# Gate tiles from one DRAM buffer per token chunk, the first of them on GpSimd's queue, and routing steps over more expert blocks

## The chip, the cores and the metric

The kernel runs on one core of a Trainium2 chip. The metric is the time of one execution on the device, in microseconds; lower is better. The profile is of one execution of the same program.

## The reference

Two layers over 512 tokens of 1024 numbers. Layer 0 mixes with a gated linear recurrence, layer 1 with attention that forgets; after each mixer stands a PEER feed-forward, which is what the change is about:

```
q = (xc @ q_w).reshape(TOKEN_CHUNK, PEER_HEADS, 2, PEER_HALF)
s1, s2 = scores of q against two sets of 128 subkeys, for 8 heads
v1, i1 = lax.top_k(s1, 16); v2, i2 = lax.top_k(s2, 16)
top_s, top_c = lax.top_k(all sums of a v1 and a v2, 16)
expert = e1 * 128 + e2                    # 16384 experts, 16 a head
g = jax.nn.softmax(top_s, axis=-1)
act = gelu(einsum('thkd,td->thk', take(expert_u, expert), xc))
out = einsum('thk,thkd->td', g * act, take(expert_v, expert))
```

Everything is float32.

## The kernel before

`peer` (L612) is called once per layer. It treats the four chunks of 128 tokens in two ways. For three of them (`nd` = 3) the experts are computed densely: for each of 128 blocks of 128 experts, the first product (u, 24 matmuls of 384 columns, names `pacc`, L334 to L336), a Gelu, a multiplication by a dense matrix of gates that is zero for experts not chosen, and the second product (v, `vacc`, L949). For the fourth chunk, GpSimd gathers the rows of the chosen experts (L855) and VectorE multiplies them (L864, L876). Every float32 operand of a matmul is split in two parts, by ScalarE (`whi`, L211) and VectorE (`wlo`, L212).

The work of one layer stands in stages:

1. Queries, scores and the search for the best 16.
2. A loop over 44 blocks of experts whose first product is computed ahead (`first_up`, L632) and kept in DRAM (`ascr`). Beside the blocks runs background work: after each block `bg.pump(GP)` gives it credit, and each step of a generator that runs takes the cost that it yields. The background is, for four chunks, `route` (L768, four steps of VectorE work per chunk, names `ge`, `j`, `e`), and then, for three chunks, `dense_gates` (L787): each has 8 groups; a group makes masks on VectorE (`p`, L829 and L832; `pg`, L840), 32 small matmuls on TensorE (`gps`, L816), copies on ScalarE (`st`, L818) and a store to the DRAM buffer `gscr` (L819).
3. A loop over the 128 blocks (L961), six blocks ahead with the first product (`expert_in`). It reads the gates back from `gscr` as gate tiles (`gtile`) of 8 blocks of experts, 1536 KB each (L919), multiplies (`gated`, L935), splits (`wh`, `wl`) and runs `expert_out`. GpSimd's gathers begin once the first gated product is there (L860).

The tile framework orders each engine's instructions by priorities that it works out while building, so an instruction may stand ahead of code that was written earlier. SP's queue loads weights (`wraw`, L148) and, before the change, all gate tiles. ScalarE's queue carries the stores of `gscr` and `ascr`. GpSimd's queue carries the gathers. A load from a DRAM tile waits for the stores to that tile.

Of the kernel before, what the change touches and what calls it, by code (L numbers as in the profile page):

```python
# [4 lines left out]
F32 = mybir.dt.float32  # L5
# [30 lines left out]
NEARLY = sum(EARLY)  # L36
PUMPS = ((4.05, 1.25), (3.75, 1.15))
AHEAD = 6
GP = 4.5
GSCALE = 32768.0  # L40
M0 = 14
M2 = 18
# [12 lines left out]
def pad(g, pool, size):  # L55

    g.nc.gpsimd.memset(pool.tile([128, size // 4], F32, name="pad", bufs=1), 0.0)
# [519 lines left out]
def stored(k):  # L577


    k -= AHEAD // 2  # L580
    n, m = NFIRST // 2, PK // 2 - AHEAD // 2
    return k >= 0 and (k + 1) * n // m > k * n // m
# [29 lines left out]
def peer(g, norm_fn, u, v, grow_fn, between, nd, cost):  # L612


    tc, nc = g.tc, g.nc
    V, A, T = nc.vector, nc.scalar, nc.tensor
    ND = nd * 128
    NB = ND // 16
    gscr = g.dram.tile([NB, 128, 128, 16], F32, name="gscr", tag="gscr")
    ascr = g.dram.tile([NFIRST, 128, ND], F32, name="ascr", tag="ascr")  # L620
    with pool(tc, name="pk", bufs=1) as pk:
        hn = pk.tile([128, D], F32, name="hn")
# [100 lines left out]
        def fold(x, last):  # L723

            n = TOPK
            while n > 2:
                V.tensor_tensor(x[:, 0:n // 2, :], x[:, 0:n:2, :], x[:, 1:n:2, :], op=OP.add)  # L727
                n //= 2
            V.tensor_tensor(last, x[:, 0, :], x[:, 1, :], op=OP.add)

        def route_half(t, q):

            if q == 0:
                routes[t] = [rt.tile([128, PH * TOPK], F32, name=f"e{w}", tag=f"e{w}", bufs=TC) for w in range(2)]
            e = routes[t]
            shp = [128, TOPK, HK]
            hs = slice(q * QH, q * QH + QH)
            ks = slice(q * HK, q * HK + HK)
            posb = rt.tile([128, HK], BF, name="posb", tag="posb")
            pin = tc.keep_in_program_order if q == 0 else lambda x: x  # L740
            pin(V.tensor_copy(posb, pos[:, t, hs].rearrange("p a b -> p (a b)")))
            f1 = rt.tile([128, QH, TOPK], F32, name="f1", tag="f1")
            pin(V.tensor_copy(f1, idxs[0][:, t, hs]))
            d1 = rt.tile([128, QH, TOPK], F32, name="d1", tag="d1")
            V.tensor_copy(d1[:, :, 0:1], f1[:, :, 0:1])
            V.tensor_sub(d1[:, :, 1:], f1[:, :, 1:], f1[:, :, :-1])
            tab = []
            for w, src in enumerate((d1, idxs[1][:, t, hs])):
                x = rt.tile(shp, BF, name=f"tab{w}", tag=f"tab{w}")
                A.activation(x.rearrange("p r (h k) -> p r h k", h=QH),  # L750
                             src.rearrange("p h r -> p r h").unsqueeze(3).to_broadcast([128, TOPK, QH, TOPK]), AF.Copy)
                tab.append(x)
            ge = rt.tile(shp, BF, name="ge", tag="ge")
            ge2 = rt.tile(shp, BF, name="ge2", tag="ge2")
            V.tensor_tensor(ge, posb.unsqueeze(1).to_broadcast(shp), thr, op=OP.is_ge)
            V.tensor_tensor(ge2, ge, row, op=OP.mult)
            V.tensor_tensor(ge, ge, tab[0], op=OP.mult)
            fold(ge, e[0][:, ks])
            yield 4.4
            j = rt.tile([128, HK], BF, name="j", tag="j")  # L760
            fold(ge2, j)
            V.tensor_sub(j, posb, j)
            V.tensor_tensor(ge, j.unsqueeze(1).to_broadcast(shp), col, op=OP.is_equal)
            V.tensor_tensor(ge, ge, tab[1], op=OP.mult)
            fold(ge, e[1][:, ks])
            yield 4.4

        def route(t):  # L768

# [17 lines left out]
        def dense_gates(t, pu, pw, psum, todo):  # L787

            e1, e2, gt = routes[t]
            tp = psum.tile([128, 4, 128], F32, name="tp", tag="tp", bufs=1)
            for i, s in enumerate((e1, e2, gt)):
                T.transpose(tp[:, i, :], s, g.ident)
            shp = [128, 128, 8]
            edup = [pu.tile(shp, F16, name=f"edup{w}", tag=f"edup{w}") for w in range(2)]
            for w in range(2):
                A.activation(edup[w], tp[:, w, :].unsqueeze(2).to_broadcast(shp), AF.Copy)
            gp = [pu.tile([128, 128], F16, name=f"gp{i}", tag=f"gp{i}") for i in range(2)]
            V.tensor_scalar(gp[0], tp[:, 2, :], GSCALE, None, op0=OP.mult)  # L800
            V.scalar_tensor_tensor(gp[1], tp[:, 2, :], GSCALE, gp[0], op0=OP.mult, op1=OP.subtract)
            gdup = []
            for i in range(2):
                d = pu.tile(shp, F16, name=f"gdup{i}", tag=f"gdup{i}")
                A.activation(d, gp[i].unsqueeze(2).to_broadcast(shp), AF.Copy)
                gdup.append(d)
            yield 1.5

            def products(n, p2, pg):
                st = pw.tile([128, 128, 16], F32, name="st", tag="st", bufs=3)  # L810
                for q in range(4):
                    gps = psum.tile([128, 4, 128], F32, name="gps", tag="sps", bufs=4)
                    for r in range(4):
                        tk_ = q * 4 + r
                        for i in range(2):
                            T.matmul(gps[:, r, :], p2[:, tk_, :, :].rearrange("p a b -> p (a b)"), pg[i][:, :, tk_, :],  # L816
                                     start=(i == 0), stop=(i == 1))
                    A.activation(st[:, :, q * 4:q * 4 + 4].rearrange("p e t -> p t e"), gps, AF.Copy, scale=1.0 / GSCALE)  # L818
                nc.scalar.dma_start(gscr[n], st)  # L819

            shp = [128, 16, 16, 8]
            it = iota_e.unsqueeze(2).to_broadcast(shp)
            for b in range(8):
                bs = slice(b * 16, b * 16 + 16)

                def spread(x):
                    return x[:, bs, :].unsqueeze(1).to_broadcast(shp)
                p2 = pw.tile(shp, F16, name="p2", tag="p2")
                V.tensor_tensor(p2, iota_e.unsqueeze(1).to_broadcast(shp),  # L829
                                edup[1][:, bs, :].unsqueeze(2).to_broadcast(shp), op=OP.is_equal)  # L830
                p1 = pu.tile(shp, F16, name="p1", tag="p1")
                V.tensor_tensor(p1, it, spread(edup[0]), op=OP.is_equal)  # L832
                yield 2.4
                if todo:
                    products(*todo.pop())
                    yield 0.1
                pg = []
                for i in range(2):
                    x = pw.tile(shp, F16, name=f"pg{i}", tag=f"pg{i}")
                    V.tensor_tensor(x, p1, spread(gdup[i]), op=OP.mult)  # L840
                    pg.append(x)
                    yield 1.15
                todo.append((t * 8 + b, p2, pg))
            if t == nd - 1:
                products(*todo.pop())
# [40 lines left out]
        with pool(tc, name="ups", bufs=1, space=PSUM) as psum:  # L886
# [6 lines left out]
            with pool(tc, name="pu", bufs=1) as pu, pool(tc, name="pw", bufs=2) as pw:  # L893
                todo = []
                bg = Background(*[route(t) for t in range(TC)], *[dense_gates(t, pu, pw, psum, todo) for t in range(nd)])
                for c in FIRST[NEARLY:]:
# [3 lines left out]
                    if c in FIRST[NEARLY + 1:NEARLY + 6:4]:  # L900
                        natural(g, psum, h, TC - 1, hn, FIRST.index(c) // (NEARLY + 5))
                    bg.pump(GP)
                bg.finish()
# [3 lines left out]
        with pool(tc, name="vw", bufs=2) as vw, pool(tc, name="vps", bufs=2, space=PSUM) as psum:  # L907
            gguard = pool(tc, name="gat", bufs=8)
            gat = gguard.__enter__()
            env["gat"], env["vw"] = gat, vw  # L910
            pad(g, vw, 384)
            g.stream.third = (vw, 2)
            bg = Background(*late)
            acc = [[psum.tile([128, 512], F32, name=f"vacc{t}{d}", bufs=1) for d in range(2)] for t in range(nd)]
            ready, ins, gts = {}, {}, {}

            def gate_tile(n):
                gts[n] = vw.tile([128, NB, 8, 16], F32, name="gtile", tag="gtile")
                nc.sync.dma_start(gts[n], gscr[:, :, n * 8:n * 8 + 8, :].rearrange("b p e t -> p b e t"))  # L919

            def expert_in(c):

                if c and c % 8 == 0:
                    gate_tile(c // 8)
                ins[c] = vw.tile([128, ND], F32, name="at2", tag="at2", bufs=AHEAD + 2)
                if stored(c // 2):
                    nc.scalar.dma_start(ins[c], ascr[FIRST.index(c)])
                else:
                    A.activation(ins[c], proj_t(g, psum, h, ND), AF.Gelu)  # L929
# [22 lines left out]
            def pump(i):  # L952
                bg.pump(cost[1] if stored(i // 2) else cost[0])

            for i in range(AHEAD):
                if i == 3:
                    gate_tile(0)
                expert_in(i)
                if i > 3:
                    gated(i - 4)()  # L960
# [425 lines left out]
```

## Time and profile before

| what | us |
|---|---|
| median of 3 runs | 3155.22 |
| lowest and highest | 3146.97, 3159.86 |
| the profiled execution, its own time | 3146.6 |
| its span, from first to last instruction | 3144.8 |
| PE busy | 3050.0 |
| VectorE (DVE) busy | 2583.9 |
| ScalarE (ACT) busy | 1457.9 |
| GpSimd (POOL) busy | 959.7 |

In the profile's rows PE is the matmul engine and PEld its weight loads; "x" is a count; what stands in brackets or after "|" is the idle time ahead of an instruction and what ended it. Each stage of layer 0 has a twin in layer 1, some 1610 us later: routing runs from 460 us to 541 and from 2071 to 2152, the dense gates from there to 692 and 2303, and the loop over 128 blocks follows.

### The profile page before, as it was taken

The numbers are of one execution on the slowest core, as the hardware profiler recorded it, in microseconds if no ns is written. First come the engines' busy times: TensorE is split into PE (matmuls) and PEld (weight loads), VectorE is DVE, ScalarE is ACT, GpSimd is POOL, SyncE is SP. The second block draws the span as 40 slices with busy tenths as digits, with TensorE's granted clock in tenths as the row PEclk, the third lists the DMA queues.
The fourth block names the chain that finished last, engine by engine and source line by source line (L and its number), as shares of the span: only waits on it lengthen the run. The fifth ranks groups of instructions, "written<-read, shape, count | busy, mean of one in ns | idle before, by whom it ended". The sixth has DMA issues, their size and how long they took to land.

```text
span 3144.8 us, 44367 instructions
## 1 busy us (share of the span) xinstructions
PE 3050.0 (97%) x16192; PEld 2681.3 (85%) x16192; DVE 2583.9 (82%) x5297; ACT 1457.9 (46%) x2109; POOL 959.7 (31%) x845
## 2 busy tenths in 40 slices
PE   6998999999999999999999999999999999999999
PEld 5876899998888888888777778899998888888887
DVE  7876899887988988888569876999869788888884
ACT  4763236883333333333458743257853333333332
POOL 1001440006644245542011102410037344544430
PEclk9998999999999999999999999999999999999999
DMA  6545334779999999997332243346699999999983
GB/s 264 155 172 170 113 131 168 268 271 400 409 377 362 365 361 355 362 343 285 126 119 82 95 143 123 104 167 222 248 359 411 360 374 340 343 340 347 355 311 117
DMA packets 304780, 818.98 MB, mean 260 GB/s; under 512 B 27824, under 2 KB 156848, under 8 KB 276016
## 3 DMA queue, kind: packets, MB, share of 16 engines
q1 hardware_dynamic: 173104, 389.83, 34.8%
q0 software_dynamic: 89408, 321.43, 26.8%
q10 hardware_dynamic: 42048, 104.88, 9.0%
q8 instruction: 127, 2.08, 0.3%
q14 instruction: 93, 0.76, 0.1%
HBM read 735.03 MB, written 81.02 MB: 259 GB/s over the span
## 4 chain that ended last, share of the span: by engine, by line
PE 60%; DVE 15%; issue 10%; DMA 6%; POOL 5%; ACT 4%; SPq 0%; POOLq 0%; DVEq 0%; ACTq 0%
PE vacc L949 22%; PE pacc L334 9%; PE pacc L336 9%; PE pacc L335 9%; POOL rows L855 4%; PE gps L816 3%; DVE wlo L212 3%; DMA wraw<-in_l_v_dram 2%; DVE rows L864 1%; DVE mw L177 1%; DVE tk L652 1%; ACT whi L211 1%; DVE ge L727 1%; DMA at<-ascr 1%; DVE idxs L651 1%
## 5 line engine op out<-in xcount | busy, mean ns | idle before, releaser
L211 ACT ACTIVATE whi<-wraw 128x1024 fp32r<-128x1024 f32 (+1 forms) x646 | 663.3, 1034 | 598.4 <-PE pacc L335 349.7
L334 PE MATMUL pacc<-hhi,whi 128*128 128x384 f32 (+1 forms) x2632 | 926.2, 352 | 8.5 <-ACT at L929 5.0
L336 PE MATMUL pacc<-hhi,wlo 128*128 128x384 f32 (+1 forms) x2632 | 921.3, 350 | 3.5 <-DVE wlo L212 3.5
L335 PE MATMUL pacc<-hlo,whi 128*128 128x384 f32 (+1 forms) x2632 | 919.6, 349 | 0.0
L212 DVE TENSOR_TENSOR wlo<-wraw,whi 128x1024 fp32r<-128x1024 f32 (+1 forms) x580 | 700.5, 1211 | 187.7 <-ACT whi L211 187.2
L949 PE MATMUL vacc<-wlo,wh 128*128 128x512 f32 x1536 | 605.2, 394 | 0.7 <-DVE wlo L212 0.7
L949 PE MATMUL vacc<-whi,wh 128*128 128x512 f32 x1536 | 602.1, 392 | 0.0
L949 PE MATMUL vacc<-whi,wl 128*128 128x512 f32 x1536 | 596.6, 388 | 0.5 <-DVE wl L942 0.4
L334 PEld LDWEIGHTS pacc<-hhi,whi 128*128 128x128 f32 x2632 | 495.9, 188 | 39.0 <-ACT at L929 5.6
L336 PEld LDWEIGHTS pacc<-hhi,wlo 128*128 128x128 f32 x2632 | 495.1, 188 | 30.2 <-DVE wlo L212 5.4
L335 PEld LDWEIGHTS pacc<-hlo,whi 128*128 128x128 f32 x2632 | 495.9, 188 | 29.2 <-issue 1.7
L939 ACT ACTIVATE wh<-at 128x384 fp32r<-128x384 f32 x256 | 134.0, 525 | 768.0 <-DVE at L935 469.2
L855 POOL DMA_INDIRECT rows<-in_l_v_dram,ei x256 | 360.5, 1408 | 382.1 <-DVE accg L876 342.9
L855 POOL DMA_INDIRECT rows<-in_l_u_dram,ei x256 | 367.9, 1437 | 264.4 <-DVE rows L864 212.5
L949 PEld LDWEIGHTS vacc<-whi,wl 128*128 128x128 f32 x1536 | 288.3, 188 | 66.1 <-DVE wl L942 1.8
L949 PEld LDWEIGHTS vacc<-whi,wh 128*128 128x128 f32 x1536 | 288.2, 188 | 61.4
L949 PEld LDWEIGHTS vacc<-wlo,wh 128*128 128x128 f32 x1536 | 288.8, 188 | 53.5 <-DVE wlo L212 1.1
L876 DVE SCALAR_TENSOR_TENSOR accg<-rows,act,accg 128x1024 f32<-128x1024 f32 x254 | 324.8, 1279 | 0.5
L864 DVE SCALAR_TENSOR_TENSOR rows<-rows,hn 128x1024 f32<-128x1024 f32 x256 | 304.8, 1219 | 12.6 <-DMA rows<-in_l_u_dram,ei 12.6
L935 DVE TENSOR_TENSOR at<-at,gtile 128x384 f32<-128x384 f32 x256 | 140.7, 552 | 131.8 <-DMA at<-ascr 122.1
L818 ACT ACTIVATE st<-gps 128x512 f32<-128x512 f32 x192 | 186.0, 1111 | 35.7 <-PE gps L816 35.7
L212 POOL TENSOR_TENSOR wlo<-wraw,whi 128x1024 fp32r<-128x1024 f32 (+1 forms) x66 | 134.9, 2054 | 192.0 <-ACT whi L211 192.0
(281 smaller groups left out, 3367.6 us busy)
## 6 DMA issues: line engine op xcount, KB each, us to landing
wraw<-in_l_uT_dram SPq DMA_DIRECT2D x128, 1024.0 KB, 7.1
wraw<-in_l_v_dram SPq DMA_DIRECT2D x128, 1024.0 KB, 9.4
gscr<-st ACTq DMA_DIRECT2D x48, 1024.0 KB, 5.1
gtile<-gscr SPq DMA_DIRECT2D x32, 1536.0 KB, 16.1
mw<-in_l_ffn_mw_dram POOLq DMA_DIRECT2D x48, 512.0 KB, 3.6
ascr<-at ACTq DMA_DIRECT2D x112, 192.0 KB, 2.9
at<-ascr ACTq DMA_DIRECT2D x112, 192.0 KB, 7.6
mw<-in_l_mix_mw_dram POOLq DMA_DIRECT2D x32, 512.0 KB, 5.7
```

Of the source, the lines that this page charges most:

```text
L211: g.nc.scalar.activation(hi, raw, AF.Copy)
L212: (eng or g.nc.vector).tensor_sub(lo, raw, hi)
L334: nc.tensor.matmul(ps, whi[:, k, :], hhi[:, k, :n], start=(k == 0), stop=False)
L335: nc.tensor.matmul(ps, whi[:, k, :], hlo[:, k, :n], start=False, stop=False)
L336: nc.tensor.matmul(ps, wlo[:, k, :], hhi[:, k, :n], start=False, stop=(k == KD - 1))
L818: A.activation(st[:, :, q * 4:q * 4 + 4].rearrange("p e t -> p t e"), gps, AF.Copy, scale=1.0 / GSCALE)
L855: i = nc.gpsimd.indirect_dma_start(out=rows, out_offset=None, in_=src, in_offset=bass.IndirectOffsetOnAxis(ap=ei[:, j:j + 1], axis=0))
L864: V.scalar_tensor_tensor(r, r, 1.0, hn, op0=OP.mult, op1=OP.mult, accum_out=act[:, j:j + 1]))
L876: tc.keep_in_program_order(V.scalar_tensor_tensor(acc, r, w, acc, op0=OP.mult, op1=OP.add))
L935: pin(V.tensor_tensor(at.rearrange("p (b t) -> p b t", t=16), at.rearrange("p (b t) -> p b t", t=16), gts[c // 8][:, :, c % 8, :], op=OP.m ...
L939: pin(A.activation(wh, at, AF.Copy))
L949: T.matmul(acc[t][d], x[:, ts], y[:, d, :], start=(i == 0 and x is wh and y is vh), stop=(i == PK - 1 and x is wl))
```

## The change

The DRAM buffer of the gates becomes three, one per chunk. A gate tile is loaded by three DMAs, one per buffer, into thirds of the same tile. The three of the first tile are issued on GpSimd's queue before the loop's first block; those of the others on SP's queue, in the code at three successive blocks. The two costs that a half of a routing step yields go from 4.4 to 5.4, and the credit per block from 4.5 to 4.85. A pad at the head of a pool grows from 384 to 512 bytes.

```diff
-GP = 4.5
+GP = 4.85
...
-    gscr = g.dram.tile([NB, 128, 128, 16], F32, name="gscr", tag="gscr")
+    gscr = [g.dram.tile([8, 128, 128, 16], F32, name=f"gscr{t}", tag=f"gscr{t}") for t in range(nd)]
...
             fold(ge, e[0][:, ks])
-            yield 4.4
+            yield 5.4
...
             fold(ge, e[1][:, ks])
-            yield 4.4
+            yield 5.4
...
-                nc.scalar.dma_start(gscr[n], st)
+                nc.scalar.dma_start(gscr[n // 8][n % 8], st)
...
-            pad(g, vw, 384)
+            pad(g, vw, 512)
...
-            def gate_tile(n):
-                gts[n] = vw.tile([128, NB, 8, 16], F32, name="gtile", tag="gtile")
-                nc.sync.dma_start(gts[n], gscr[:, :, n * 8:n * 8 + 8, :].rearrange("b p e t -> p b e t"))
+            def gate_tile(n, t, queue):
+
+                if t == 0:
+                    gts[n] = vw.tile([128, NB, 8, 16], F32, name="gtile", tag="gtile")
+                queue.dma_start(gts[n][:, t * 8:t * 8 + 8],
+                                gscr[t][:, :, n * 8:n * 8 + 8, :].rearrange("b p e t -> p b e t"))
 
             def expert_in(c):
 
-                if c and c % 8 == 0:
-                    gate_tile(c // 8)
+                if c >= 8 and c % 8 < nd:
+                    gate_tile(c // 8, c % 8, nc.sync)
...
+            for t in range(nd):
+                gate_tile(0, t, nc.gpsimd)
             for i in range(AHEAD):
-                if i == 3:
-                    gate_tile(0)
                 expert_in(i)
```

How the instructions move, at three places of layer 0 (layer 1 has the same). VectorE where routing ends and the dense gates begin, before; `p` and `pg` are the masks of the first group, `wlo` a split for a block of experts, `ge`, `e` and `ei` the end of routing:

```order
L212 TENSOR_TENSOR wlo<-wraw,whi 128x1024
L727 TENSOR_TENSOR ge<-ge 128x512
L832 TENSOR_TENSOR p_5301<-iota_f,edup_5287 128x2048
L727 TENSOR_TENSOR ge<-ge 128x256
L800 TENSOR_SCALAR gp_5291<-tp 128x128
L727 TENSOR_TENSOR ge<-ge 128x128
L801 SCALAR_TENSOR_TENSOR gp_5292<-tp,gp_5291 128x128
L729 TENSOR_TENSOR e_5077<-ge 128x64
L829 TENSOR_TENSOR p_5299<-iota_f,edup_5288 128x2048
L783 SCALAR_TENSOR_TENSOR ei<-e_5076,e_5077 128x128
L840 TENSOR_TENSOR pg_5337<-p_5301,gdup_5295 128x2048
L840 TENSOR_TENSOR pg_5339<-p_5301,gdup_5297 128x2048
```

The same place on VectorE now:

```order
L727 TENSOR_TENSOR ge<-ge 128x128
L729 TENSOR_TENSOR e_5113<-ge 128x64
L783 SCALAR_TENSOR_TENSOR ei<-e_5112,e_5113 128x128
L212 TENSOR_TENSOR wlo<-wraw,whi 128x1024 x2
L832 TENSOR_TENSOR p_5369<-iota_f,edup_5355 128x2048
L800 TENSOR_SCALAR gp_5359<-tp 128x128
L829 TENSOR_TENSOR p_5367<-iota_f,edup_5356 128x2048
L801 SCALAR_TENSOR_TENSOR gp_5360<-tp,gp_5359 128x128
L840 TENSOR_TENSOR pg_5405<-p_5369,gdup_5363 128x2048
L829 TENSOR_TENSOR p_5409<-iota_f,edup_5356 128x2048
L840 TENSOR_TENSOR pg_5407<-p_5369,gdup_5365 128x2048
```

The masks of the first group now follow the end of routing, and from routing's start to the second `pg` VectorE has 19 splits and 3 `p` where it had 17 and 2. On TensorE, 48 more matmuls of `pacc` (two blocks of experts) stand ahead of the first gate product; the last gate products stand ahead of the same block as before.

SP's queue where the loop over the 128 blocks begins, before; `wraw` are weights, of the first product (uT) and of the second (v):

```order
L148 DMA wraw<-in_l_uT_dram 128x2048 x27
L919 DMA gtile<-gscr 128x24x128
L148 DMA wraw<-in_l_v_dram 128x2x1024 x2
L148 DMA wraw<-in_l_uT_dram 128x2048
L919 DMA gtile<-gscr 128x24x128
```

The same place on SP's queue now:

```order
L148 DMA wraw<-in_l_uT_dram 128x2048 x27
L148 DMA wraw<-in_l_v_dram 128x2x1024
L148 DMA wraw<-in_l_uT_dram 128x2048
L921 DMA gtile<-gscr_2301 128x8x128
L148 DMA wraw<-in_l_v_dram 128x2x1024
L921 DMA gtile<-gscr_2302 128x8x128
L921 DMA gtile<-gscr_2303 128x8x128
```

The first tile has left this queue; two weight loads stand ahead of the second tile's first piece.

GpSimd at the same place, now (before, the copy of L860 follows the memset):

```order
L57 MEMSET pad 128x128
L921 DMA gtile<-gscr_2301 128x8x128
L921 DMA gtile<-gscr_2302 128x8x128
L921 DMA gtile<-gscr_2303 128x8x128
L860 COPY act<-at_7452 128x1
L855 DMA rows<-in_l_u_dram,ei 128x1024 x128
```

The three pieces stand between the memset and the copy that opens the gathers.

## The prediction

> **What bounds the kernel now.** I read the page's busy shares first, then who the matmul engine waits for, then the stretches where it waits.
>
> ```profile
> PE 3050.0 (97%) x16192; PEld 2681.3 (85%) x16192; DVE 2583.9 (82%) x5297; ACT 1457.9 (46%) x2109; POOL 959.7 (31%) x845
> ...
> PE gps L816 <- DVE pg L840: 9.8, 4, 4.0
> PE pacc L334 <- ACT at L929: 5.0, 2, 3.5
> ```
>
> PE is busy 97% of the span, so a change that leaves its work alone can only win back its gaps. The two waits, added over both layers, are among its longest, and both lie where the diff works. The first is at the end of the routing steps, where the first gate product (gps) waits for VectorE; the second is where the gate products end and the expert loop starts. The stretches around them, with the columns us, then busy us of PE, PEld, DVE, ACT, POOL, then granted clock, DMA share and GB/s:
>
> ```profile
> 460.00:541.30 81.30, 76.57 (x448) 76.14 (x447) 80.34 (x249) 53.74 (x68) 0.00 (x0) 0.99 0.46 161
> 541.30:692.20 150.90, 150.76 (x1337) 144.68 (x1337) 135.39 (x122) 124.02 (x147) 0.18 (x1) 0.98 0.69 258
> 692.20:724.00 31.80, 27.53 (x173) 26.85 (x171) 11.87 (x14) 16.11 (x22) 1.89 (x2) 0.95 0.97 344
> 2070.60:2151.90 81.30, 76.53 (x448) 76.10 (x447) 80.34 (x250) 53.80 (x68) 0.00 (x0) 0.99 0.46 161
> 2303.10:2330.00 26.90, 24.59 (x165) 23.91 (x163) 9.61 (x10) 14.96 (x20) 1.43 (x2) 1.00 1.01 365
> ...
> 540.00:550.00 10.00, 8.83 (x66) 8.51 (x66) 10.00 (x10) 6.08 (x8) 0.00 (x0) 0.71 0.52 179
> 720.00:730.00 10.00, 10.00 (x43) 9.26 (x44) 4.01 (x6) 4.45 (x8) 6.38 (x7) 0.83 1.06 379
> ```
>
> In the routing stretch (first and fourth row, one per layer) VectorE is full, 80.34 of 81.30, and PE loses 4.7 us. In the gate stretch (second row) PE is full and VectorE has 15.5 us free. So work is badly divided between two neighbouring stretches. In the start of the expert loop PE loses 4.3 us in layer 0 and 2.3 in layer 1.
>
> **Routing steps, costed at 5.4 for 4.4, with 4.85 credit for 4.5 per block.** The table of order shows that the first gate product comes after two more expert blocks, while the last one stays where it was. What the handover costs now (PE in order of time, idle before each row in brackets), and what an expert block costs:
>
> ```profile
> 540.30 0.27 PE L816 MATMUL gps<-pg,p 128*128 128x128 f16 x1 [4.00 <-DVE pg L840]
> 541.44 3.46 PE L816 MATMUL gps<-pg,p 128*128 128x128 f16 x31 [0.87 <-DVE pg L840]
> 549.47 1.96 PE L816 MATMUL gps<-pg,p 128*128 128x128 f16 x32
> 555.50 1.96 PE L816 MATMUL gps<-pg,p 128*128 128x128 f16 x32
> ...
> 696.06 0.33 PE L334 MATMUL pacc<-hhi,whi 128*128 128x384 f32 x1
> 710.10 0.33 PE L334 MATMUL pacc<-hhi,whi 128*128 128x384 f32 x1
> ```
>
> A block with its 32 gate products takes 6.03 us (549.47 to 555.50). The first one took 9.17 (540.30 to 549.47): 3.14 too many, since it waits 0.87 more and its products run in 3.46 for 1.96 at a clock of 0.71. With the 4.00 before it the handover costs 7.1 us per layer. From 696.06 to 710.10 there are 27 groups of three matmuls, so a block of eight groups takes 14.04 / 27 x 8 = 4.16 us.
>
> Afterwards PE reaches the handover 2 x 4.16 = 8.3 us later. VectorE has before it two more splits (wlo) and one more comparison (p):
>
> ```profile
> L212 DVE TENSOR_TENSOR wlo<-wraw,whi x24: 1215/1219/1227, 543.6 to 688.7; 128x1024 fp32r<-128x1024 f32 x24
> ...
> DVE wlo L212 <- ACT whi L211: 7.3, 5, 3.2
> DVE p L829 <- PE gps L816: 3.4, 4, 1.4
> DVE pg L840 <- PE gps L816: 2.9, 3, 1.9
> DVE p L832 <- ACT edup L798: 1.1, 1, 1.1
> ```
>
> That is 3 x 1.22 = 3.7 us, so VectorE gains 4.6 on a wait of 4.87 and 0.3 remains. Short waits such as this show no fall of the clock, so the slow products go too: 7.1 - 0.3 = 6.8 us.
>
> Next, what is late: the gate stretch is two blocks shorter with the same 24 groups of products. PE needs 150.9 - 3.1 - 8.3 = 139.5 us there, VectorE's work is 135.4 - 3.7 = 131.7, ScalarE's stays below its 124.0. VectorE also waits, in the four rows above: 8.4 us for ScalarE and 6.3 for PE. If only the waits for ScalarE recur, it needs 140.1, which is 0.6 more than PE. If all recur, it needs 146.4 and 6.9 of the gain is gone; if none do, nothing is lost. I take 0.6, since waits for PE are what vanishes when VectorE is the later one. Gain per layer 6.2, ends 0 and 7.1; both layers 12.4.
>
> **First gate tile on GpSimd's queue, in three pieces.** Today it stands on SP's queue ahead of the first weights of the second product (v):
>
> ```profile
> 699.89 6.44 DMA gscr<-st
> ...
> 706.51 0.38 SPq L919 DMA_DIRECT2D gtile<-gscr  x1
> 706.94 5.48 SPq L148 DMA_DIRECT2D wraw<-in_l_v_dram  x2
> 767.63 10.74 SPq L148 DMA_DIRECT2D wraw<-in_l_v_dram  x1
> ...
> 715.01 0.56 DVE L935 TENSOR_TENSOR at<-at,gtile 128x384 f32<-128x384 f32 x1 [8.80 <-DMA gtile<-gscr]
> 717.55 2.00 ACT L211 ACTIVATE whi<-wraw 128x1024 fp32r<-128x1024 f32 x2 [8.84 <-DMA wraw<-in_l_v_dram]
> ```
>
> SP waits until the last gate store has landed (699.89 + 6.44 = 706.3), and only then the weights go. Their issues, two in 5.48 us, are themselves slow behind a tile of 1536 KB. ScalarE, in order, then stands 8.84 us before the split of v, behind it the reading of a PSUM bank (at), behind that PE: 3.5 us, then a clock of 0.83 for 10 us, 1.7 more. In the new order v and one more load stand ahead of any gate tile on SP, so they need not wait for the store, and v goes at about 702.4 in the old times, 4.5 earlier; with its 10.5 us to landing unchanged it lands at 713.0, and with the slow issue gone near 708. A bank read at 712 then finds ScalarE free. Layer 0 gains 3.5 + 1.7 = 5.2; layer 1 has 2.3 us idle there, 0.8 of it waits of the gate products for ScalarE that stay, so 1.5. Ends: 0 and 6.7 together. I take 6.7, and give back 2.0 because the weights then run into DMA engines that are already full:
>
> ```profile
> 740.00:750.00 10.00, 9.69 (x50) 8.63 (x50) 10.00 (x17) 2.80 (x4) 8.44 (x6) 1.00 1.02 419
> ```
>
> The three pieces on GpSimd: its own work there is in these rows.
>
> ```profile
> 691.12 0.18 POOL L57 MEMSET pad<- 128x96 f32 x1 [235.16 <-DVE p L829]
> 721.61 0.36 POOL L860 COPY act<-at 128x1 f32<-128x1 f32 x1 [30.31 <-DVE at L935]
> 725.55 0.94 POOL L855 DMA_INDIRECT rows<-in_l_u_dram,ei  x1 [0.30 <-issue]
> 749.90 1.99 POOL L855 DMA_INDIRECT rows<-in_l_u_dram,ei  x1 [0.30 <-issue]
> ...
> L170 POOL DMA_DIRECT2D mw<-in_l_ffn_mw_dram x48: 527/528/600, 101.1 to 1868.7; - x48
> ```
>
> GpSimd is idle for 30 us between the memset and the copy ahead of the row gathers, so the pieces hide there. The memset still waits for VectorE's last p, so pieces 0 and 1 leave only some 15 us ahead of the last store's landing, not when their chunks end. Piece 2 waits for that landing. Nothing but the gathers stands behind it, and they need the first tile anyway. A load of 128 rows costs GpSimd 0.53 us; a piece has 1024 short rows, so between 0.53 and 8 x 0.53 = 4.2 us. I take about 2, nearer the row; with the last store landing near 700 and the 8.4 us that the whole tile now takes to land (706.51 to 714.9, by the wait of the first gated product), piece 2 is there by 711, and PE comes to it at about 714. Later gate tiles become three DMAs that stand side by side on SP: two more issues of 0.38 us each, on an idle queue, costed at nothing. The larger pad and the names of the DRAM buffers cost nothing; the cover of the pad is that idle time.
>
> The rule that speaks against this queue is in the Trainium skill, "SBUF — State Buffer", section on the three doors: while VectorE runs an instruction that takes both ports, GpSimd cannot write descriptors, and its DMAs start late. The gathers above went from 0.94 us with VectorE idle to 1.99 with it full, so the trace agrees in direction. By the page's own example, 620 ns becoming 3100, the three pieces would cost GpSimd five times 0.53 each, 8 us by estimate, still inside its idle 30.
>
> **Sum.** 12.4 + 6.7 - 2.0 = 17.1 us against the profiled execution's 3146.6 (span 3144.8), so 3129.5. That execution is 0.3% under the median of the three runs, 3155.2; the same gain from the median gives 3138.
>
> **Rivals.**
> *The wait is spread, not removed (0.18).* VectorE's waits all recur in the shorter gate stretch and PE stops in small pieces. For it: only 15.5 us of slack there, and 14.7 of waits. Against: 6.3 of those are waits for PE. Both layers then keep 0.2 each, and 4.7 of the start remain: 3150.
> *The pieces are late (0.11).* GpSimd pays 4.2 x 1.99 / 0.94 = 8.9 us for piece 2 in place of 2, on the path: last store's landing at 706.3 - 6.2 = 700.1, plus 8.9, plus the 8.4 to landing, gives 717.4. PE without its wait comes to the tile's first product at about 714, less 1.1 for VectorE and ScalarE (0.56 and 0.5): 4.5 late per layer, and the clock's 1.7. The start then gains nothing in layer 0 and loses 5 in layer 1: about 3148. Against it: GpSimd's idle 30 us and a third of the bytes.
> *Three DMAs per later tile starve PE (0.07), slower.* Behind a later gate tile a weight load took 10.74 us to issue (the row at 767.63). If the two extra DMAs delay the 28 later tiles' next weights by more than the buffers hold, each costs PE something; above 17.1 / 28 = 0.6 us per tile the change loses, and at 1.2 it gives 3138 + 34 = 3172. Against it, between 860 and 1450 ScalarE waits for weights only this much, and PE not at all:
>
> ```profile
> ACT whi L211 <- DMA wraw<-in_l_uT_dram: 6.9, 3, 4.1
> ACT whi L211 <- DMA wraw<-in_l_v_dram: 4.3, 1, 4.3
> ```
>
> **Chances and range.** My forecast holds 0.64: 3138, its own range 3128 to 3147 (half of the handover's or of the start's gain more or less). 0.5%, about what a measurement of this kernel can tell from no change, is 15.8 us or 3139.4, nearly at my number; so I split the case there: 0.45 below, 0.19 above, since the sum counts only gaps that the rows show and gives 2.0 back already. The first two rivals end within 0.5%, which makes faster 0.45, same 0.19 + 0.18 + 0.11 = 0.48, slower 0.07. The range reaches to the first two rivals and, with runs spread by 13 us, to 3157 above; below, all three ends taken at their best give 7.1 x 2 + 6.7 = 21 and some scatter: 3124.
>
> **What would show it.** Right: the wait of gps for pg under 1 us and a clock near 1.00 in the ten microseconds of the handover; PE's 24 groups starting two blocks later and ending some 6 us earlier; no wait of PE for at (L932 now); v issued without a gap behind a gate tile. Wrong: PE waits for wlo or pg inside the gate stretch, or DVE's first gated product waits for gtile past the sixth block. Most likely to spoil it is the thin margin of VectorE in the gate stretch.

## The result, and the profile after

The changed kernel took 3179.8 us (median of 6 runs, 3170.96 to 3187.99) against 3153.47 before: ratio 1.0086, 95% interval 1.0064 to 1.0109. It is slower by about 27 us, where 17 us less were forecast. The profiled execution took 3176.7, its span is 3174.9 against 3144.8.

First the busy line and the groups of the second product on the page of before, then the same of the changed kernel (groups: count, then busy us and mean ns of one, then idle time before them):

```profile
L949 PE MATMUL vacc<-wlo,wh 128*128 128x512 f32 x1536 | 605.2, 394 | 0.7 <-DVE wlo L212 0.7
L949 PE MATMUL vacc<-whi,wh 128*128 128x512 f32 x1536 | 602.1, 392 | 0.0
L949 PE MATMUL vacc<-whi,wl 128*128 128x512 f32 x1536 | 596.6, 388 | 0.5 <-DVE wl L942 0.4
```

```profile
PE 3074.9 (97%) x16192; PEld 2680.7 (84%) x16192; DVE 2581.7 (81%) x5297; ACT 1463.9 (46%) x2113; POOL 967.2 (30%) x851
...
L952 PE MATMUL vacc<-whi,wh 128*128 128x512 f32 x1536 | 607.0, 395 | 3.3 <-ACT whi L211 3.3
L952 PE MATMUL vacc<-wlo,wh 128*128 128x512 f32 x1536 | 606.7, 395 | 1.2 <-DVE wlo L212 1.2
L952 PE MATMUL vacc<-whi,wl 128*128 128x512 f32 x1536 | 607.1, 395 | 0.8 <-DVE wl L945 0.8
```

This pair carries most of the result. PE has the same 16192 matmuls and is busy 24.9 us longer (3050.0 before), with the same mean clock of 0.988 in both executions. So the loss does not show mainly as waits: the matmuls themselves follow each other more slowly. The three groups of vacc add 17 us (1803.9 to 1820.8), and where they had three different means, 394, 392 and 388, they now have one.

The waits that the prediction spoke of, after:

```profile
PE pacc L334 <- ACT at L932: 8.0, 2, 5.0
...
PE pacc L336 <- DVE wlo L212: 6.9, 7, 3.4
...
PE gps L816 <- DVE pg L840: 4.6, 8, 1.0
```

The handover from routing (gps for pg) went from 9.8 to 4.6 us with no wait above 1.0, as forecast. The wait at the start of the expert loop (pacc for at) grew from 5.0 to 8.0. Of the 6.9 us of waits for wlo, 1.3 lie in each layer's gate stretch and the rest, with the longest of 3.4, at the starts of the two loops. The stretches (us, busy of PE, PEld, DVE, ACT, POOL, then clock, DMA share, GB/s):

```profile
460.00:543.50 83.50, 83.50 (x490) 83.38 (x489) 82.26 (x243) 57.86 (x71) 0.00 (x0) 1.00 0.50 172
543.50:691.80 148.30, 144.14 (x1329) 136.71 (x1328) 134.01 (x120) 125.01 (x146) 2.05 (x3) 1.00 0.69 260
691.80:724.00 32.20, 29.24 (x154) 28.22 (x154) 10.84 (x12) 14.83 (x23) 4.90 (x6) 0.95 1.04 372
...
540.00:550.00 10.00, 9.12 (x75) 8.84 (x74) 10.00 (x11) 8.59 (x10) 0.00 (x0) 1.00 0.58 213
```

PE is now full through routing (83.50 of 83.50), and the clock at the handover is 1.00 where it was 0.71. The gate stretch, full before (150.76 of 150.90), now loses 4.2 us.

To see where a difference arises, the starts of the same matmul were subtracted in the two traces, stage by stage. Positive is later than before; each column is one execution, and the experiments' labels are told below:

```
stage                     after   e2     e3     e5     e6     e9
routing to handover, L0   -8.1   -8.2   -8.2   +0.4   +0.4   -8.1
dense gates, L0           +5.2   +3.2   +2.9   -0.7   -0.6   +4.7
first 16 blocks, L0      +10.1   +3.1   +9.8   +0.4  +10.4   +3.8
blocks 16 to 80, L0       +6.5    0.0   +0.5   +6.5   +0.1   -0.6
routing to handover, L1   -8.6   -8.6   -8.6    0.0    0.0   -8.6
dense gates, L1          +10.3  +10.0   +6.6   +0.4   +0.7   +8.5
first 16 blocks, L1       +7.7   -0.1   +0.6   +0.4   +3.3   -1.6
later blocks, L1          +8.2   +2.6   +0.3   +9.7    0.0   -2.1
whole span               +30.2   -0.1   +1.6  +15.7  +12.8   -4.0
```

(A block is counted here as 42 matmuls, 24 of pacc and 18 of vacc, from the first vacc on. Since 56 of the 128 blocks have no pacc in the loop, "16 blocks" reach in truth to about the 21st, and "80" to about the 106th. "Dense gates" reach to the first vacc. Stages with little in them are left out.)

The row of the handover needs care. The pacc matmuls compared there stand behind the first 32 gate products before, and ahead of them after. Those products take 1.96 us, so some 2.0 of each 8.1 and 8.6 is work put off, not won, and it comes back in the row below. At equal work the handover won 6.1 and 6.6 us, 12.7 in all. The gate stretch, up to its last product, gave back 3.2 and 3.3; the other 5.0 of layer 1's 10.3 arise between the last gate product and the first vacc. A further 17.8 us were lost in the first blocks of the loops, and 14.7 in the rest of the loops, where no wait shows at all.

### The profile page after: what moved, and what is told of

It reads as the page before. It is cut to its first block, busy times and chain, and to the rows that moved or that the text cites. A ratio compares the mean times of both kernels' runs of the same rounds, so it can differ in the third digit from the quotient of the medians.

```text
span 3174.9 us, 44511 instructions
## 1 busy us (share of the span) xinstructions
PE 3074.9 (97%) x16192; PEld 2680.7 (84%) x16192; DVE 2581.7 (81%) x5297; ACT 1463.9 (46%) x2113; POOL 967.2 (30%) x851
## 4 chain that ended last, share of the span: by engine, by line
PE 67%; DVE 18%; DMA 6%; ACT 4%; issue 4%; POOL 1%; SPq 0%; DVEq 0%; ACTq 0%; POOLq 0%
PE vacc L952 29%; PE pacc L334 10%; PE pacc L336 9%; PE pacc L335 9%; DVE wlo L212 3%; DMA wraw<-in_l_v_dram 2%; PE gps L816 2%; DMA rows<-in_l_u_dram,ei 2%; DVE rows L864 2%; DVE ge L727 1%; DVE pg L840 1%; DVE mw L177 1%; DVE tk L652 1%; ACT whi L211 1%; DVE idxs L651 1%
## 5 line engine op out<-in xcount | busy, mean ns | idle before, releaser
L952 PE MATMUL vacc<-whi,wl 128*128 128x512 f32 x1536 | 607.1, 395 | 0.8 <-DVE wl L945 0.8
L942 ACT ACTIVATE wh<-at 128x384 fp32r<-128x384 f32 x256 | 134.0, 525 | 767.7 <-DVE at L938 416.4
L864 DVE SCALAR_TENSOR_TENSOR rows<-rows,hn 128x1024 f32<-128x1024 f32 x256 | 305.5, 1221 | 14.3 <-DMA rows<-in_l_u_dram,ei 14.1
```

Of the source, the lines that this page charges most:

```text
L864: V.scalar_tensor_tensor(r, r, 1.0, hn, op0=OP.mult, op1=OP.mult, accum_out=act[:, j:j + 1]))
L942: pin(A.activation(wh, at, AF.Copy))
L952: T.matmul(acc[t][d], x[:, ts], y[:, d, :], start=(i == 0 and x is wh and y is vh), stop=(i == PK - 1 and x is wl))
```

## The experiments

Nothing in the prediction explains a slower pace with no wait. One edit that it had costed at nothing can: a pad at the head of the pool in which the loop's tiles lie. In the built program, wh and wl (the stationary operands of vacc) begin at byte 173824 of each partition before, a multiple of 256; with the larger pad they begin 128 bytes higher. So do the gate tiles, the buffers `at2`, the third weight buffer and, behind them all, the rows that GpSimd gathers. Four kernels took the change apart, all on one chip beside 29 runs of the kernel before.

**Pad alone (e1).**

```diff
-            pad(g, vw, 384)
+            pad(g, vw, 512)
```

> The kernel before with one number changed: the pad is 512 bytes in place of 384, so every later tile of that pool lies 128 bytes higher. Theory A (the place of a tile in SBUF sets the matmul's pace): the 4608 matmuls of the second product go from 228.9 ns apart to 233.3 as in the changed kernel's trace, 4608 x 4.4 ns = 20.3 us, so about 3174 against 3153.5 (ratio 1.006), and in the trace all three kinds of vacc stand 233 ns apart. Theory B (the loss is all in the DMA queues at the start of the expert loop, and the slower pace comes from their traffic): 3153.5, ratio 1.000, and 229 ns.

Measured 3183.36 against 3148.35 us, ratio 1.0114 (1.0097 to 1.0130): 35.0 us, all of the change's loss and more. Vacc went to 233.3 ns, as theory A said; theory B, which puts the whole loss in the queues, fell. The groups of vacc on its page:

```profile
L949 PE MATMUL vacc<-whi,wl 128*128 128x512 f32 x1536 | 607.0, 395 | 4.1 <-DVE wl L942 4.1
L949 PE MATMUL vacc<-wlo,wh 128*128 128x512 f32 x1536 | 606.7, 395 | 1.3 <-DVE wlo L212 1.3
L949 PE MATMUL vacc<-whi,wh 128*128 128x512 f32 x1536 | 606.7, 395 | 0.8 <-ACT whi L211 0.8
```

But the 20.3 us of the pace are not all of the loss.

**The change with the old pad (e2)** (the same edit the other way).

> The changed kernel with the pad back at 384 bytes. Theory A: 20.3 us less than the changed kernel's 3179.8, so about 3160 (ratio 1.002 against the kernel before), vacc at 229 ns. Theory B: 3180, ratio 1.0086, vacc at 233 ns.

3147.04, ratio 1.0006 (0.9995 to 1.0018): the rest of the change, taken together, makes no difference. Vacc is back at 229, 226 and 232 ns.

**Routing costs alone (e3)** (`GP` 4.85, both yields 5.4).

> The kernel before with only the routing costs of 5.4 and the credit of 4.85 per block. By the two traces the handover wins 8.1 us in layer 0 and 8.6 in layer 1, and the end of the dense gates gives 3.3 and 4.3 back. If nothing else takes it away: 3153.5 - 9.1 = 3144 (ratio 0.997). If the start of the expert loop is paced by DMA engines that are full whatever PE's lead, the lead is lost there: 3151 to 3155 (ratio 0.999 to 1.0005), with v landing at the same time as before near 790 us.

3144.26, ratio 0.9992 (0.9984 to 1.0001). Of the 9.1 us that the two traces promised, 3 to 4 are left (by the ratio and by the medians), and the interval touches 1. In the table the lead at the handover is there in each kernel with these costs (-8.1 to -8.6), and the gates' end and the loop's first blocks take most of it back.

**Gates part alone (e4)** (buffers, pieces and queues as changed; pad, costs and credit as before).

> The kernel before with only the three DRAM buffers of gates, the three pieces per tile and the first tile on GpSimd's queue; costs, credit and pad as before. Theory A and three issues per tile that hold up SP's queue: what is left of the changed kernel's loss, 3179.8 - 20.3 + 9.1 = 3169 (ratio 1.005), lost at the start of the expert loop in both layers, behind the second to fourth gate tile. The prediction's reading (first weights earlier, pieces hidden): 3147 (ratio 0.998).

3151.03, ratio 1.0012 (1.0003 to 1.0021): a loss of 2.7 us, not the gain of the prediction and not the 3169 that I expected after the first comparison, since most of what I had put down to the pieces, at the loop's starts, belonged to the pad. (Its profiled execution, 3166.8, is far above its median and is not read here.)

Two questions were left: what the pad does beyond the pace, and what place would be best. The next two kernels each move a part of what the pad moves, and put the rest back to its old place modulo 512, the gathered rows in both.

**Stationary operands alone, 128 bytes higher (e5).**

```diff
+                if c == 0:
+                    nc.gpsimd.memset(vw.tile([128, 32], F32, name="pad2", bufs=1), 0.0)
                 wh = vw.tile([128, ND], F32R, name="wh", tag="wh", bufs=5)
...
                 wl = vw.tile([128, ND], F32R, name="wl", tag="wl", bufs=5)
+                if c == 0:
+                    nc.gpsimd.memset(vw.tile([128, 96], F32, name="pad3", bufs=1), 0.0)
```

> The kernel before with wh and wl alone 128 bytes higher (a second pad ahead of them and a third behind, so that what DMAs write, at2, gtile, wraw and rows, keeps its place modulo 512). Pad alone cost 35.0 us, of which 4608 x 4.4 ns = 20.3 are pace and the rest was lost at the two starts of the expert loop. Theory A1 (place of the stationary operand, all of it): ratio 1.011, about 3183, since a slower second product also meets the full DMA engines differently. Theory A2 (two effects: the pace by wh and wl, the starts of the loop by the places that DMAs write to): 3148.4 + 20.3 = 3169, ratio 1.0065. If the place of wh and wl has no part in it: 3148, 229 ns.

3164.69 against 3147.2, ratio 1.0054 (1.0037 to 1.0071): 17.5 us. The groups of vacc on its page:

```profile
L953 PE MATMUL vacc<-whi,wl 128*128 128x512 f32 x1536 | 606.0, 395 | 0.2 <-DVE wl L946 0.2
L953 PE MATMUL vacc<-wlo,wh 128*128 128x512 f32 x1536 | 605.4, 394 | 0.0
L953 PE MATMUL vacc<-whi,wh 128*128 128x512 f32 x1536 | 605.3, 394 | 0.0
```

All three are at 394 to 395 ns, with 0.2 us of waits among them. In the table the loop's first 16 blocks cost it 0.4 us per layer, and the blocks after them 6.5 and 9.7: pace and nothing else.

**DMA targets alone, 128 bytes higher (e6)** (pad 512, and a second pad of 384 ahead of wh and wl).

> The reverse: pad 512, so that at2, gtile and the third wraw lie 128 bytes higher, and a second pad of 384 ahead of wh and wl, which with the gathered rows then stand as before modulo 512. Theory A1: 3148, ratio 1.000, vacc at 229 ns. Theory A2: vacc at 229 ns, and the 15 us of the loop starts lost all the same: about 3163, ratio 1.0047. If the moving operand's or the targets' place alone did it: 3183.

3157.68 against 3147.2, ratio 1.0029 (1.0018 to 1.0041): 10.5 us. Theory A2 holds in kind (it had put 15 us on the starts): vacc is back at 229, 226 and 232 ns from start to start, the later blocks cost nothing, and the first 16 blocks lose 10.4 and 3.3. The two parts, 17.5 and 10.5, add up to 28 of the pad's 35. The other 7 are near the edge of what the intervals leave, and neither kernel moved the gathered rows; more on these below.

**Gate tiles alone (e12), and the third weight buffer alone (e13), 128 bytes higher.** In the first, each gate tile lies 128 bytes into a buffer 512 bytes longer; in the second, the same was done to the loop's own two weight buffers (a third of the loads).

```diff
-                gts[n] = vw.tile([128, NB, 8, 16], F32, name="gtile", tag="gtile")
+                gts[n] = vw.tile([128, NB * 128 + 128], F32, name="gtile", tag="gtile")[:, 32:NB * 128 + 32].rearrange("p (b e t) -> p b e t", e=8, t=16)
```

> The kernel before with the gate tiles alone 128 bytes higher (each buffer 512 bytes longer, the tile 128 bytes into it); all else at the old places modulo 512. Moving at2, gtile and the third wraw together cost 10.5 us, with 3% fewer GB/s at the same DMA share at the loop's starts. If the 512-byte pieces of a gate tile that begin off a multiple of 256 bytes are what is slow: most of the 10.5, ratio 1.002 to 1.003. If it is the weights' 8 KB rows (or the gathers' company with them): 1.000.

> The kernel before with only the third weight buffer (wraw in the loop's pool, 2 buffers, a third of the loads) 128 bytes higher, all else at the old places modulo 512. If long rows are slow off a multiple of 256: 1.002 to 1.003 and fewer GB/s at the same DMA share; if only the short pieces of the gate tiles are: 1.000.

3156.04 and 3149.31 against 3148.9: ratios 1.0021 (1.0012 to 1.0030) and 1.0002 (0.9993 to 1.0011). So it is the gate tiles. Their DMA writes pieces of 512 bytes (8 blocks by 16 numbers), a weight load rows of 8 KB (uT) or 4 KB (v). The same 60 us in the loop's start of layer 1, in order before, gate tiles and others moved, gate tiles alone, weight buffers alone, stationary operands alone:

```profile
2330.00:2390.00 60.00, 59.47 (x295) 52.86 (x294) 53.86 (x84) 20.84 (x33) 48.41 (x32) 1.00 1.04 413
```

```profile
2330.00:2390.00 60.00, 55.88 (x274) 50.01 (x273) 48.71 (x74) 23.02 (x33) 40.86 (x29) 0.97 1.05 396
```

```profile
2330.00:2390.00 60.00, 56.38 (x276) 50.33 (x275) 48.82 (x74) 22.94 (x33) 39.57 (x29) 0.97 1.05 394
```

```profile
2330.00:2390.00 60.00, 59.28 (x297) 53.08 (x296) 52.22 (x81) 21.36 (x31) 47.39 (x32) 1.00 1.04 410
```

```profile
2330.00:2390.00 60.00, 59.23 (x294) 52.75 (x295) 52.34 (x81) 21.55 (x32) 45.71 (x32) 1.00 1.04 410
```

The DMA engines are equally full (1.04 or 1.05), but with the gate tiles moved they carry 394 and 396 GB/s instead of 410 to 413, and PE loses 3 to 4 us of the 60. The packets on the DMA queues show it without the mix of transfers in a window. Times of one packet in ns, from each run's trace; "128" and "64" tell how far off a multiple of 256 the target lies:

```
                                    before  e5    e13   e12   e6    e1    after  e8
gate tiles begin at                    0     0     0    128   128   128   128    64
512-byte packets of them, mean       27.3  27.4  27.3  29.7  29.9  30.3  29.9   30.3
gathered rows begin at                 0     0     0     0     0    128   128    64
4 KB packets of them, 720 to 860 us:
  time that nine in ten keep to       159   159   159   159   159   171   171    169
```

The gate tiles' packets take 9 to 11% longer wherever the tiles are moved, and only there. `at2` was not moved alone, but in e6 its packets of 1536 bytes take 65 ns at the median as before. The second half of the table holds what e5 and e6 left out: where the gathered rows are moved too, with the pad alone, in the changed kernel and with the pad of 448 below, their packets take longer as well. So the rows are the likely place of the missing 7 us. No kernel moved them alone, and so what they cost is not shown.

**The routing costs with other pads, 128 (e7) and 448 (e8).**

> The routing costs of the change on the kernel before, with a pad of 128 bytes: wh and wl begin at 0 modulo 512 in place of 256. If only a place off a multiple of 256 bytes is slow: vacc at 228.9 ns as with 384 and the time of the routing part alone, 3144 (ratio 0.9992). If rows that begin at a multiple of 512 are read faster (one row of weights is 512 bytes): 226 ns or less for all three kinds, 4608 x 3 = 14 us less, 3131 (ratio 0.9945). If the distance to whi and wlo (at 320 modulo 512) sets it: some value of its own between 226 and 234 for each kind.

> The same with a pad of 448 bytes: wh and wl begin at 320 modulo 512, exactly as whi and wlo. If only a multiple of 256 is good: 233 ns and what the pad cost, 3144 + 35 = 3179 (ratio 1.010). If the distance to whi and wlo counts and equal places are worst or best: away from 233 on one side, 4608 ns for each ns, 3144 plus or minus some 15.

3144.09 against 3147.2, ratio 0.9989 (0.9978 to 0.9999), and 3160.28, ratio 1.0035 (1.0021 to 1.0049). A pad of 128 gives the pace of 384 to the tenth of a nanosecond, so 0 and 256 modulo 512 are alike. With 448 the expectation of 3179 missed: the pace is the best so far, 227.9 ns, and the whole loss is at the loop's starts (first 16 blocks +14.3 and +10.7 in its trace), where the gate tiles, and with them all else that DMAs write there, now begin at 64 modulo 256.

**Routing costs, and wh and wl alone at the place that was best (e9)** (pad 384; second and third pad of 64 and 448 bytes around them).

> The routing costs of the change, pad 384, and wh and wl alone moved up by 64 bytes, to 320 modulo 512; at2, gtile, wraw and rows keep their places modulo 512. If the second product's pace goes by the place of wh and wl and the loss of the pad 448 was all in what DMAs write: vacc at 227.9 ns on average as there, no loss at the loop's starts, 4608 x 1.0 = 4.6 us under the routing part alone: ratio 0.9977, about 3140. If the places act otherwise: 3144 or more, 0.999 to 1.003.

3139.55 against 3149.54, ratio 0.9958 (0.9944 to 0.9972): 10 us less than the kernel before by the medians, 13 by the ratio, and so faster than both kernels. The pace is 227.9 ns as said, and the starts of the loop lose no more than with the routing costs alone. Routing part and pace together make 7 to 9 us; what is beyond that is not explained. Its groups:

```profile
L953 PE MATMUL vacc<-whi,wl 128*128 128x512 f32 x1536 | 600.4, 391 | 1.1 <-DVE wl L946 1.1
L953 PE MATMUL vacc<-wlo,wh 128*128 128x512 f32 x1536 | 600.1, 391 | 0.7 <-DVE wlo L212 0.6
L953 PE MATMUL vacc<-whi,wh 128*128 128x512 f32 x1536 | 597.4, 389 | 0.0
```

**The gates part, in two.** First tile alone on GpSimd's queue, whole, ahead of the loop (e10), and all tiles in three pieces on SP from one DRAM buffer (e11):

```diff
-                if i == 3:
-                    gate_tile(0)
+            gate_tile(0, nc.gpsimd)
```

```diff
-                nc.sync.dma_start(gts[n], gscr[:, :, n * 8:n * 8 + 8, :].rearrange("b p e t -> p b e t"))
+                nc.sync.dma_start(gts[n][:, t * 8:t * 8 + 8],
+                                  gscr[t * 8:t * 8 + 8, :, n * 8:n * 8 + 8, :].rearrange("b p e t -> p b e t"))
```

> The kernel before with only the first gate tile on GpSimd's queue, in one piece and from the one DRAM buffer; later tiles, costs and pad as before. The prediction's second step: 6.7 - 2.0 = 4.7 us less, ratio 0.9985, v issued without a gap. If the start of the loop is paced by full DMA engines, the earlier start is lost again at the second and fourth gate tile: ratio 1.000. If GpSimd's piece brings its cost with it: 1.001 (the three DRAM buffers and pieces together cost 2.7 us with the old costs of routing and 2.8 with the new).

> The kernel before with only the tiles cut: three DMAs per gate tile, all on SP's queue, from the one DRAM buffer. The prediction: two more issues per tile, nothing, ratio 1.000. Its third rival: above 0.6 us per tile and 28 tiles, 17 us or more, ratio 1.005. If it is what the gates part costs: 2.8 us, ratio 1.001, with SP held up by the second or third piece while weights stand behind it at the loop's start.

3153.03 against 3149.54, ratio 1.0005 (0.9994 to 1.0016), and 3157.17, ratio 1.0016 (1.0005 to 1.0026). The first tile's queue makes no difference; the pieces cost 5 us by the ratio. In the pieces' trace (an execution of 3163.0 us, 6 above the median) one wait of PE in layer 1 alone takes 7.5 us. SP's queue there and ScalarE's split of the uT weights, before and with pieces:

```profile
2369.56 0.37 SPq L919 DMA_DIRECT2D gtile<-gscr  x1
2375.27 11.07 SPq L148 DMA_DIRECT2D wraw<-in_l_v_dram  x1
2386.44 1.36 SPq L148 DMA_DIRECT2D wraw<-in_l_uT_dram  x1
...
2402.69 1.06 ACT L211 ACTIVATE whi<-wraw 128x1024 fp32r<-128x1024 f32 x1 [0.43 <-DMA wraw<-in_l_uT_dram]
```

```profile
2375.38 15.16 SPq L920 DMA_DIRECT2D gtile<-gscr  x3
2390.64 4.25 SPq L148 DMA_DIRECT2D wraw<-in_l_v_dram  x1
2394.99 1.27 SPq L148 DMA_DIRECT2D wraw<-in_l_uT_dram  x1
...
2417.10 1.06 ACT L211 ACTIVATE whi<-wraw 128x1024 fp32r<-128x1024 f32 x1 [9.02 <-DMA wraw<-in_l_uT_dram]
```

and PE's longest wait in the start of that loop, with pieces:

```profile
PE pacc L334 <- ACT whi L211: 7.5, 1, 7.5
```

A gate tile took one issue of 0.37 us, and it was the load of v behind it whose issue took 11.07; the three pieces hold SP for 15.16 us. The weights of the first product (uT) behind them are issued at 2394.99 instead of 2386.44, but 5.8 of these 8.6 us this execution was late already (by the starts of the vacc matmuls just ahead), so the held queue accounts for 2.7. From issue to ScalarE's split the uT weights then take 22.1 us instead of 16.3, another 5.9. PE waits for just these weights, by way of the split. Why their transfer takes longer is not shown.

## Why the prediction was wrong

**The failed step** is one clause: "The larger pad and the names of the DRAM buffers cost nothing". It was bounded by nothing and covered by the wrong thing (GpSimd's idle time, which covers the memset). The pad alone measured 35.0 us, more than every other term together. No rival held it either, and the range ended at 3157. The rows needed were on the page: three groups of vacc with the same shape and three means, 388, 392 and 394 ns, show that the time of a matmul depends on something other than its shape.

**Handover, 12.4 us.** The mechanism was right: no wait above 1.0, clock 1.00, 6.1 and 6.6 us won at equal work (7.1 less 0.3 were forecast for each layer). The give-back was mis-sized: 0.6 us per layer for the shorter gate stretch, where 3.2 and 3.3 were measured. VectorE's waits between 543.5 and 691.8 after:

```profile
DVE wlo L212 <- ACT whi L211: 4.8, 3, 3.2
DVE p L829 <- PE gps L816: 4.3, 4, 1.8
DVE p L832 <- ACT edup L798: 2.3, 1, 2.3
DVE pg L840 <- PE gps L816: 0.6, 2, 0.4
```

I had taken it that waits for PE vanish when VectorE is the later engine; 4.9 of the 6.3 us came back. With 7.1 for ScalarE and 134.0 of work VectorE needs 146.0 us there, close to the 146.4 of the case "if all recur", and PE loses 4.2, 0.9 of it at the handover itself. The rest shows the prediction's own sign of being wrong: from 640 us on PE waits 1.6 us for pg, 1.3 for wlo and 0.4 for ScalarE. So the rival of the spread wait ran beside the forecast, not instead of it. Measured alone, the step is worth 3 to 4 us, and nothing at the edge of its interval.

**First gate tile, 6.7 - 2.0 us.** The first part came as said: v is issued at 698.57 with no gap, ahead of any gate tile on SP's queue. Rows of SP, GpSimd, ScalarE, PE and VectorE, after:

```profile
698.57 0.42 SPq L148 DMA_DIRECT2D wraw<-in_l_v_dram  x1
699.09 0.47 SPq L148 DMA_DIRECT2D wraw<-in_l_uT_dram  x1
699.66 0.49 SPq L921 DMA_DIRECT2D gtile<-gscr  x1
702.39 5.17 SPq L148 DMA_DIRECT2D wraw<-in_l_v_dram  x1
...
688.81 1.84 POOL L921 DMA_DIRECT2D gtile<-gscr  x2 [0.59 <-ACT st L818]
707.61 0.88 POOL L921 DMA_DIRECT2D gtile<-gscr  x1 [16.96 <-issue]
...
710.21 1.06 ACT L211 ACTIVATE whi<-wraw 128x1024 fp32r<-128x1024 f32 x1 [6.98 <-DMA wraw<-in_l_v_dram]
...
711.70 0.45 PE L334 MATMUL pacc<-hhi,whi 128*128 128x384 f32 x1 [2.96 <-ACT at L932]
...
716.30 0.56 DVE L938 TENSOR_TENSOR at<-at,gtile 128x384 f32<-128x384 f32 x1 [3.77 <-DMA gtile<-gscr]
```

But v landed only at 710.2, 11.6 us after its issue (10.5 taken) on DMA engines that are full (1.04); and PE, early by the handover's gain, stood there from 708.7. So both sides of this wait had moved, and the wait stayed: 3.0 and 5.0 us in the two layers, where 3.5 and 1.5 had been. I moved the transfer and left its partner where it was. The third piece went out at 707.61, no earlier than the whole tile before (706.51): it waits for the last gate store, whose landing I put 6.2 us earlier, at 700.1. The last gate product is only some 4 us earlier (691.19 in the changed trace). The store, issued at 696.0, took over 11 us where it had taken 6.44, with weights and two pieces issued ahead of it; that these held it up is not shown by a run of its own. Alone, the step gives a ratio of 1.0005.

**GpSimd's pieces, 2 us each, hidden.** They took 0.9 us each (1.84 for two, 0.88), hidden as said. The tile was there at 716.3, not 711. VectorE was busy for only 10.84 of the 32.20 us there, so the rule cited against this queue had little to act on. Nor do the two gathers compared in the prediction, 0.94 and 1.99 us, settle that rule: in the same trace the gathers at 731.76 and 746.39, beside a busy VectorE, took 0.94 as well.

**Later tiles in three pieces, nothing.** A small cost, not none: with the cut alone the kernel is slower by 0.16%, 5 us. The third rival had the place and the mechanism (weights behind pieces on SP) but put 0.6 to 1.2 us on each of 28 tiles; the trace shows the wait where the DMA engines are full, at one tile, and not at the later ones, and only a part of it is the held queue. The rival's time of 3172 came close to the measured one for a reason that was not its own.

**The sum.** Routing about -4, gates part +2.7, pad +35 make +34 against the measured 27; the intervals (20 to 34 for the change) leave that open to the last few us.

## What to carry to other kernels

A pad, a new tile or another order of allocation moves every tile behind it, and this costs time without any wait: compare the busy time of equal groups and the means of groups of one shape before reading waits. Price such an edit by what it does to the places of a matmul's stationary operand and of DMA targets written in short pieces, 1.1% here for 128 bytes. And a lead won ahead of a tight stage and of one paced by full DMA engines is mostly lost there: of some 13 us won at the handovers, 3 to 4 were left with the routing costs alone.

## What the runs showed of the hardware that was not expected

The pace of a float32 matmul with 128 x 128 weights and 512 columns goes by the place of the stationary operand. From start to start, without waits, whi and wlo (moving) always at 64 modulo 256:

```
wh, wl modulo 256    whi,wh   whi,wl   wlo,wh   mean, ns
0 (before, e7)        229.2    225.9    231.6    228.9
128 (after, e1, e5)   233.3    233.4    233.4    233.3
64 (e8, e9)           226.9    228.8    228.1    227.9
```

The weight loads themselves do not show it: 187 to 188 ns in the changed kernel's page, 188 in the loop before. Whether the place counts by itself or against that of the moving operand is not told apart. The Trainium skill, "TensorE: Matmul & The Clock Gate", section "Step-by-step: what each phase is for", says that PE reads the moving operand and the weights through two independent ports, so that "Loading the next tile's weights doesn't steal SBUF read bandwidth from the running matmul"; it says nothing of where operands lie. By the two ports alone one would expect no change, and here, for float32, the pace changed by 2.4% between two places of the weights.

A DMA that writes 512-byte pieces is slower when they begin 128 bytes off a multiple of 256: 29.7 ns for 27.3 for a packet, 394 GB/s for 413 at nearly the same share, and 7.1 us for the gate tiles alone. For the weights' rows of 4 and 8 KB, moved in a third of the loads, no loss was measured (1.0002, 0.9993 to 1.0011); the gathers' rows of 4 KB take longer in the traces in which they were moved. The Trainium skill, "DMA: Bandwidth & Descriptors", section "How a descriptor splits into AXI transactions", has the rule that fits: a descriptor is cut at multiples of 256 bytes, and one that begins off them pays for a first transaction that it uses in part. By estimate from it, 20 beats for 16 in a piece of 512 bytes, and 260 for 256 in a row of 8 KB. That is 25% more for the piece, where the packets' mean grew by 9 to 11%. The page tells it of reads; the runs show the loss where such pieces are written. By the same estimate a start at 64 would be the milder one (18 beats), while the packets' mean is 30.3 ns at 128 (e1) and at 64 (e8).
